# Four modulation vectors of an encoder kernel: one-column products against selector products of split halves

## The chip, the cores and the metric

The kernel runs on one core of a Trainium2 chip. Its engines work side by side, each with its own queue: the PE (TensorE, matrix products into PSUM; its weight loads are listed apart as PEld), DVE (VectorE), ACT (ScalarE), POOL (GpSimd) and SP, whose queue issues nearly all transfers (DMA) between the chip's memory and the on-chip buffers. The metric is the device time of one execution in microseconds (us); lower is better.

## The reference

The reference is a trunk of two layers on 256 tokens of width 2048, all in float32. Each layer makes six vectors of 2048 from the conditioning vector c:

```
mod = (silu(c) @ w_mod[l] + b_mod[l])  ->  shift_m, scale_m, gate_m, shift_f, scale_f, gate_f
h = layer_norm(x) * (1 + scale_m) + shift_m          # first modulation
y = concat(four mixers of h @ w_in[l]) @ w_out[l]
x = layer_norm(ALPHA * x + (1 + gate_m) * y)
h = layer_norm(x) * (1 + scale_f) + shift_f          # second modulation
y = conv_ffn(h, ...)                                  # up (2 x 5632), short conv, silu, down
x = layer_norm(ALPHA * x + (1 + gate_f) * y)
```

w_mod of a layer is 2048 x 12288, so the modulation is a product of one row with a large matrix: much memory traffic for little arithmetic.

## The kernel before

**Products.** The weights arrive in float32 and are split into two float32r halves, high and low: ACT casts to the high half `whi` (line 455), DVE subtracts it from the raw weights to get the low half `wlo` (line 456). The activations are split in the same way (`split`, lines 475 and 476). Three products then stand in for one of float32: high by high, high by low, low by high. Some weights are left whole (`wexact`, loaded at line 433) and multiplied in float32. The raw weights use four buffers (`raw`), the halves four buffers of 128 x 1024 under the tag `whi` and four under `wlo`; whole weights take buffers of these two tags in turn, or spare ones (`slot`).

**Stages.** Layer 0 begins with its first modulation in pieces, mixed with its first projections. Each layer then runs the mixers, the output projection (`out_proj`, PSUM tiles `o`), the up projection (`g_c`, `v_c`) and the down projection (`out_proj` again, PSUM tiles `d`). `out_proj` works in three chunks of 1024, 512 and 512 columns. In the last chunk the products of the last four units are kept back and run for token tile 0 first and for token tile 1 second, so that the norm of token tile 0 can begin while the PE still works on token tile 1. `second` (lines 734 to 762) is that norm for token tile 0, `norm` the one for token tile 1. `to_hT` then casts the normalised tokens (`xn`), transposes them on the PE (line 594) and applies scale and shift (`hF`). Its cast carries a dependency on the instructions that finished the scale and the shift (`MOD_BY`). `first_group` runs the first products of the next stage on whole weights: its first unit of weights is loaded ahead of the kept-back products, the three others behind them.

**Modulation.** DVE accumulates each vector over 16 steps: an accumulator of 128 x 2048 (`macc`) gets the raw block of w_mod times one column of silu(c) (`mod_step`, line 250). What is left is the sum over the 128 partitions. `mod_stream` feeds these steps between the units of the main products at rates fixed by hand (`RATES`). When a vector's steps are through, it waits in the list `late` until `settle` sums it:

- gates go to `gate_rows`: split halves, multiplied by a block of ones;
- layer 1's second shift and scale go to `mod_rows`: split halves multiplied by selectors (128 x 4 with one column of ones, `onesR` behind its first 128 columns), which put the sum of column block j into row j of one PSUM tile `ps_row`. The row is copied (`mrow`, line 227), turned by four transposes (line 230), and added to the bias on DVE (line 232);
- all others go to `mod_cols`: a product of the bias columns with the identity, then one float32 product with a single column of ones per block of 128, with the accumulator's block as the stationary operand (`ps_mod`, line 83), and a copy on ACT (lines 207 and 86).

The vectors that are needed at the start of a norm (`WITH_NORM`: layer 0's second shift and scale, layer 1's first shift and scale) are not settled inside the stream but by `need`, called from `before()` at the end of `out_proj`'s last chunk:

```
if before is not None:
    before()
for t in range(2):
    finish(t, state["ps"], c0)
    (norm if t == 1 or then is None else second)(t)
```

Layer 0's second shift and scale are accumulated in two parts: 12 blocks of 128 columns ahead of this place, the other four later.

**Order.** The program states the work in this order; a planner then fixes each engine's queue ahead of the run from its own cost estimates, taking an instruction earlier where an engine would stand idle and its inputs and a buffer are at hand. All products of the kernel are recorded under line 83, so the tiles' names tell them apart.

Of the kernel before, what the change touches and what calls it, by code (L numbers as in the profile page):

```python
# [8 lines left out]
F32R = mybir.dt.float32r  # L9
# [4 lines left out]
P = 128  # L14
# [4 lines left out]
KT = D // P  # L19
# [12 lines left out]
SHIFT_M, SCALE_M, GATE_M, SHIFT_F, SCALE_F, GATE_F = range(6)  # L32
# [22 lines left out]
def encoder_kernel(ctx: ExitStack, tc: tile.TileContext, A: dict, consts: bass.AP, out: bass.AP):  # L55
# [5 lines left out]
    splitp = ctx.enter_context(tc.tile_pool(name="splitp", bufs=4))  # L61
# [11 lines left out]
    def tmp_tile(name):  # L73
        return tmpp.tile([P, 512], F32, tag="tmp", name=name)

    def ms_tile(name):
        return msp.tile([P, 512], F32, tag="ms", name=name)
# [4 lines left out]
    def mm(o, lhsT, rhs, start, stop):  # L82
        pe.matmul(o, lhsT, rhs, start=start, stop=stop, skip_group_check=True)  # L83
# [21 lines left out]
    onesR = keep.tile([P, P + 16], F32R, name="onesR")  # L105
# [50 lines left out]
    bcol = []  # L156
# [41 lines left out]
    def mod_cols(l, m, k0, acc):  # L198

        n = acc.shape[1] // P  # L200
        ps = ms_tile("ps_mod")
        mm(ps[:, 0:n], ident, bcol[l][:, m * KT + k0 : m * KT + k0 + n], True, False)
        for j in range(n):
            mm(ps[:, j : j + 1], acc[:, j * P : (j + 1) * P], ones[:, 0:1], False, True)
        cols = keep.tile([P, n], F32, name=f"mod_{l}_{m}_{k0}")
        if m in (SHIFT_M, SHIFT_F):
            done = act.copy(cols, ps[:, 0:n])
        else:
            done = ident_act(cols, ps[:, 0:n], 1.0, ones[:, 0:1])
        for j in range(n):  # L210
            MOD[(l, m, k0 + j)] = cols[:, j : j + 1]
            MOD_BY[(l, m, k0 + j)] = done.ins.name

    def halves(acc, c0):
        hi = splitp.tile([P, 1024], F32R, tag="whi", name="mhi")
        lo = splitp.tile([P, 1024], F32R, tag="wlo", name="mlo")
        split((hi, lo), acc[:, c0 : c0 + 1024])
        return [(hi[:, i * 512 : (i + 1) * 512], lo[:, i * 512 : (i + 1) * 512]) for i in range(2)]

    def mod_rows(l, m, acc):  # L220

        ps = ms_tile("ps_row")
        for j, pair in enumerate(halves(acc, 0) + halves(acc, 1024)):
            for n, part in enumerate(pair):
                mm(ps[0:4, :], onesR[:, P + 4 * j : P + 4 * j + 4], part, j + n == 0, j + n == 4)
        row = tmp_tile("mrow")
        act.copy(row[0:4, :], ps[0:4, :])
        ps = ms_tile("ps_mod")
        for i in range(4):
            pe.transpose(ps[:, 4 * i : 4 * i + 4], row[0:4, i * P : (i + 1) * P], ident[0:4, 0:4])  # L230
        cols = keep.tile([P, KT], F32, name=f"mod_{l}_{m}")
        done = dve.scalar_tensor_tensor(
            out=cols.rearrange("p (i j) -> p i j", i=4),
            in0=ps[:, 0:KT].rearrange("p (i j) -> p i j", i=4),
            scalar=0.0 if m == SHIFT_F else 1.0,
            in1=bcol[l][:, m * KT : (m + 1) * KT].rearrange("p (j i) -> p i j", i=4),
            op0=ALU.add,
            op1=ALU.add,
        )
        for k in range(KT):  # L240
            at = 4 * (k % 4) + k // 4
            MOD[(l, m, k)] = cols[:, at : at + 1]
            MOD_BY[(l, m, k)] = done.ins.name
# [39 lines left out]
    def gate_rows(l, m, acc):  # L283

        g = keep.tile([P, D], F32, tag="gate", name=f"gate_{l}_{m}")
        for h in range(2):
            for i, (hi, lo) in enumerate(halves(acc, h * 1024)):
                c0 = h * 1024 + i * 512
                ps = ms_tile("ps_gate")
                mm(ps, onesR[:, 0:P], hi, True, False)  # L290
                mm(ps, onesR[:, 0:P], lo, False, True)
                ident_act(g[:, c0 : c0 + 512], ps, 1.0, ones[:, 0:1])
        GATE[(l, m)] = g
# [5 lines left out]
    def settle(i=0):  # L299
        l, m, acc, k0, k1 = late.pop(i)  # L300
        if m in (GATE_M, GATE_F):
            gate_rows(l, m, acc)
        elif (l, m) in ((1, SHIFT_F), (1, SCALE_F)):
            mod_rows(l, m, acc)
        else:
            mod_cols(l, m, k0, acc[:, k0 * P : k1 * P])

# [15 lines left out]
    def mod_stream(order):  # L323
# [4 lines left out]
        for l, m in order:  # L328
# [10 lines left out]
            while len(late) >= 2:  # L339
                if late[0][:2] in WITH_NORM:  # L340
                    yield
                else:
                    settle()
# [5 lines left out]
            for kt in range(KT):  # L349
                raw = raw_tile("wmod")  # L350
                nc.sync.dma_start(out=raw[:, :w], in_=A["w_mod"][l, kt * P : (kt + 1) * P, m * D : m * D + w])
                if kt == KT - 1 and m in (GATE_M, GATE_F):
                    row = raw_tile("brow")
                    nc.sync.dma_start(out=row[0:1, :], in_=A["b_mod"][l : l + 1, m * D : (m + 1) * D])
                mod_step(acc[:, :w], raw[:, :w], kt, kt == 0)
                if kt == KT - 1:
                    if m in (GATE_M, GATE_F):
                        dve.tensor_tensor(out=acc[0:1, :], in0=acc[0:1, :], in1=row[0:1, :], op=ALU.add)
                    late.append((l, m, acc, 0, k1))
                yield  # L360
                if kt == 1 and late and late[0][:2] not in WITH_NORM:
                    settle()
# [16 lines left out]
    def need(l, m, k1=KT):  # L379
        while (l, m, k1 - 1) not in MOD and (l, m) not in GATE:  # L380
            at = [i for i, x in enumerate(late) if x[:2] == (l, m) and x[4] == k1]
            if at:
                settle(at[0])
            else:
                assert next(mods, "end") != "end"
# [87 lines left out]
    def split(dst, src):  # L473
        hi, lo = dst[:2]
        act.copy(hi, src)  # L475
        dve.tensor_tensor(out=lo, in0=src, in1=hi.bitcast(F32), op=ALU.subtract)  # L476
# [1142 lines left out]
```

## Time and profile before

| | |
|---|---|
| median of 3 runs | 2282.78 us (2282.72 to 2288.62) |
| profiled execution, its own time | 2281.42 us |
| its span | 2279.7 us |
| mean granted PE clock | 0.991 |
| PE, DVE, ACT busy | 98%, 78%, 48% of the span |
| memory traffic | 605.21 MB, mean 265 GB/s |

The times are those of whole executions; the profile is one execution of its own, and the span is what its trace covers. In rows of the timeline the first number is the start in us from the span's start, the second the length, then engine, line, operation, output and inputs by tile names, and the number of instructions merged; in brackets stands the idle time of the engine before them and what ended it. Rows of groups give the shortest, median and longest duration in ns. "PEclk" is the granted clock of the PE as a share of full speed. Under each of the four calls in question: the product of the bias and the one-column products of layer 0's second shift ran from 340.88, its scale's from 393.30, layer 1's first shift's from 1038.82, its first scale's from 1118.58.

### The profile page before, as it was taken

The page shows a single profiled execution, that of the slowest core. Times are in us where ns is not written, and L with a number is a line of the kernel's source. Part 1 is how long each engine was busy: PE and PEld are TensorE (multiplying, and loading weights), DVE is VectorE, ACT ScalarE, POOL GpSimd, SP SyncE. Part 2 cuts the span into 40 slices and gives each one's busy share as a digit, 9 for nine tenths or more (in the row PEclk, how much of TensorE's full clock was granted, in tenths as well). Part 3 has the DMA queues.
Part 4 walks back from the last instruction along what each step waited for, and adds up shares of the span by engine and source line. Part 5 has one row for each costly group of instructions (what it writes and reads, how often), then busy time and mean ns, then how long its engine had stood idle before and what let it go on. Part 6 is the DMA issues. An engine that isn't in the chain of part 4 may idle for free.

```text
span 2279.7 us, 31503 instructions
## 1 busy us (share of the span) xinstructions
PE 2238.7 (98%) x12387; PEld 1934.8 (85%) x12387; DVE 1773.3 (78%) x2183; ACT 1098.2 (48%) x1644; POOL 35.1 (2%) x65
## 2 busy tenths in 40 slices
PE   7999999999999999999999999999999999999998
PEld 5788886798888888888789999889888888888886
DVE  5778988888888888988977899787676565565776
ACT  3356641354455444544454434545544454454553
POOL 0011000000000000000000000000000000000000
PEclk9999999999999999999999999999999999999999
DMA  9999699778888888898777677775666555555554
GB/s 349 385 373 359 256 328 349 249 278 314 311 307 315 314 312 327 303 346 302 273 236 254 201 242 250 271 273 177 240 240 215 192 185 197 191 185 194 187 191 148
DMA packets 228717, 605.21 MB, mean 265 GB/s; under 512 B 14660, under 2 KB 27188, under 8 KB 210900
## 3 DMA queue, kind: packets, MB, share of 16 engines
q1 hardware_dynamic: 227784, 602.30, 74.3%
q8 instruction: 97, 1.59, 0.3%
q0 software_dynamic: 784, 0.90, 0.1%
q14 instruction: 52, 0.43, 0.0%
HBM read 601.05 MB, written 2.10 MB: 265 GB/s over the span
## 4 chain that ended last, share of the span: by engine, by line
PE 88%; DVE 7%; DMA 2%; ACT 2%; issue 1%; POOL 0%; SPq 0%; DVEq 0%; ACTq 0%; POOLq 0%
PE g_c L83 22%; PE v_c L83 22%; PE d L83 20%; PE o L83 7%; PE D_c L83 3%; PE C_c L83 3%; PE B_c L83 2%; PE U_c L83 1%; PE E L83 1%; PE E_c L83 1%; DVE wlo L456 1%; PE ps_mod L83 1%; PE V L83 1%; DVE qacc L250 1%; DVE macc L250 1%
## 5 line engine op out<-in xcount | busy, mean ns | idle before, releaser
L455 ACT CAST whi<-wraw 128x1024 fp32r<-128x1024 f32 (+1 forms) x632 | 643.4, 1043 | 753.1 <-PE g_c L83 217.0
L456 DVE TENSOR_TENSOR wlo<-wraw,whi 128x1024 fp32r<-128x1024 f32 (+1 forms) x632 | 750.5, 1214 | 294.3 <-ACT whi L455 273.2
L83 PE MATMUL d<-whi,a 128*128 128x512 f32 x1344 | 390.3, 391 | 0.9 <-ACT whi L455 0.9
L250 DVE SCALAR_TENSOR_TENSOR macc<-wmod,cact,macc 128x2048 f32<-128x2048 f32 (+2 forms) x174 | 353.9, 2034 | 41.5 <-DMA wmod<-in_w_mod_dram 40.8
L83 PE MATMUL v_c<-hT,whi 128*128 128x512 f32 (+1 forms) x1456 | 343.1, 383 | 0.0
L83 PE MATMUL g_c<-hT,whi 128*128 128x512 f32 (+1 forms) x1344 | 313.5, 380 | 0.0
L83 PEld LDWEIGHTS v_c<-hT,whi 128*128 128x128 f32 x1456 | 264.6, 189 | 48.5
L83 PEld LDWEIGHTS d<-whi,a 128*128 128x128 f32 x1344 | 253.4, 189 | 54.5 <-ACT whi L455 2.2
L83 PEld LDWEIGHTS g_c<-hT,whi 128*128 128x128 f32 x1344 | 243.4, 189 | 43.5 <-DVE second L1436 0.4
L83 PE MATMUL d<-wlo,a 128*128 128x512 f32 x672 | 234.8, 392 | 1.6 <-DVE wlo L456 1.6
L83 PE MATMUL v_c<-hT,wlo 128*128 128x256 f32 x1400 | 190.7, 283 | 0.0
L83 PEld LDWEIGHTS v_c<-hT,wlo 128*128 128x128 f32 x1400 | 183.1, 191 | 6.6
L83 PE MATMUL g_c<-hT,wlo 128*128 128x256 f32 x1280 | 175.8, 283 | 0.0
L83 PEld LDWEIGHTS g_c<-hT,wlo 128*128 128x128 f32 x1280 | 168.2, 191 | 5.9
L83 PEld LDWEIGHTS d<-wlo,a 128*128 128x128 f32 x672 | 126.7, 189 | 30.1 <-DVE wlo L456 3.6
L475 ACT CAST a<-g 128x512 fp32r<-128x512 f32 x132 | 80.8, 619 | 91.1 <-PE d L83 89.4
L83 PE MATMUL o<-whi,a 128*128 128x512 f32 x384 | 111.3, 395 | 0.2 <-ACT whi L455 0.2
L476 DVE TENSOR_TENSOR a<-g,a 128x512 fp32r<-128x512 f32 x132 | 87.7, 684 | 9.2 <-ACT a L475 9.2
L250 DVE SCALAR_TENSOR_TENSOR qacc<-wmod,cact,qacc 128x1024 f32<-128x1024 f32 (+1 forms) x75 | 80.3, 1071 | 12.2 <-DMA wmod<-in_w_mod_dram 9.9
L83 PEld LDWEIGHTS o<-whi,a 128*128 128x128 f32 x384 | 72.7, 190 | 16.4 <-issue 0.7
L83 PE MATMUL D_c<-hT,whi 128*128 128x256 f32 x432 | 83.0, 292 | 2.4 <-ACT hT L475 1.6
L83 PEld LDWEIGHTS D_c<-hT,whi 128*128 128x128 f32 x432 | 69.5, 197 | 4.8 <-ACT hT L475 1.7
(370 smaller groups left out, 2619.1 us busy)
## 6 DMA issues: line engine op xcount, KB each, us to landing
wraw<-in_ffn_w_up_dram SPq DMA_DIRECT2D x168, 1024.0 KB, 5.0
wmod<-in_w_mod_dram SPq DMA_DIRECT2D x134, 1024.0 KB, 6.8
wraw<-in_ffn_w_down_dram SPq DMA_DIRECT2D x88, 1024.0 KB, 5.1
wraw<-in_w_in_dram SPq DMA_DIRECT2D x33, 1024.0 KB, 6.1
wmod<-in_w_mod_dram SPq DMA_DIRECT2D x64, 512.0 KB, 9.4
wraw<-in_w_out_dram SPq DMA_DIRECT2D x26, 1024.0 KB, 6.9
wmod<-in_w_mod_dram SPq DMA_DIRECT2D x32, 768.0 KB, 7.5
wexact<-in_w_in_dram SPq DMA_DIRECT2D x46, 512.0 KB, 7.9
```

What stands on the lines that cost most here:

```text
L83: pe.matmul(o, lhsT, rhs, start=start, stop=stop, skip_group_check=True)
L250: i = dve.scalar_tensor_tensor(out=acc, in0=w, scalar=col, in1=acc, op0=ALU.mult, op1=ALU.add)
L455: act.copy(hi[:, :m], r)
L456: i = dve.tensor_tensor(out=lo[:, :m], in0=r, in1=hi[:, :m].bitcast(F32), op=ALU.subtract)
L475: act.copy(hi, src)
L476: dve.tensor_tensor(out=lo, in0=src, in1=hi.bitcast(F32), op=ALU.subtract)
```

## The change

`mod_rows` takes a number n of 512-column blocks (4 or 3), `halves` a width. `settle` now sends every late vector that starts at block 0 and is not a gate through `mod_rows`. That moves four calls from `mod_cols`: layer 1's first shift and scale (16 blocks each) and the first 12 blocks of layer 0's second shift and scale. The last four blocks of the latter and layer 0's first modulation stay with `mod_cols`. Per moved call the bias product, the 16 or 12 one-column products and the copy on ACT go; two casts and two subtractions (the second of 512 columns for 12 blocks), eight or six selector products, a copy of 4 x 512, four transposes and one addition on DVE come.

```diff
--- before.py
+++ after.py
@@ -211,18 +211,19 @@
             MOD[(l, m, k0 + j)] = cols[:, j : j + 1]
             MOD_BY[(l, m, k0 + j)] = done.ins.name
 
-    def halves(acc, c0):
-        hi = splitp.tile([P, 1024], F32R, tag="whi", name="mhi")
-        lo = splitp.tile([P, 1024], F32R, tag="wlo", name="mlo")
-        split((hi, lo), acc[:, c0 : c0 + 1024])
-        return [(hi[:, i * 512 : (i + 1) * 512], lo[:, i * 512 : (i + 1) * 512]) for i in range(2)]
-
-    def mod_rows(l, m, acc):
+    def halves(acc, c0, width=1024):
+        hi = splitp.tile([P, 1024], F32R, tag="whi", name="mhi")[:, :width]
+        lo = splitp.tile([P, 1024], F32R, tag="wlo", name="mlo")[:, :width]
+        split((hi, lo), acc[:, c0 : c0 + width])
+        return [(hi[:, i : i + 512], lo[:, i : i + 512]) for i in range(0, width, 512)]
+
+    def mod_rows(l, m, acc, n=4):
 
         ps = ms_tile("ps_row")
-        for j, pair in enumerate(halves(acc, 0) + halves(acc, 1024)):
-            for n, part in enumerate(pair):
-                mm(ps[0:4, :], onesR[:, P + 4 * j : P + 4 * j + 4], part, j + n == 0, j + n == 4)
+        parts = [x for c0 in range(0, n * 512, 1024) for x in halves(acc, c0, min(1024, n * 512 - c0))]
+        for j, pair in enumerate(parts):
+            for i, part in enumerate(pair):
+                mm(ps[0:4, :], onesR[:, P + 4 * j : P + 4 * j + 4], part, j + i == 0, j + i == n)
         row = tmp_tile("mrow")
         act.copy(row[0:4, :], ps[0:4, :])
         ps = ms_tile("ps_mod")
@@ -230,14 +231,14 @@
             pe.transpose(ps[:, 4 * i : 4 * i + 4], row[0:4, i * P : (i + 1) * P], ident[0:4, 0:4])
         cols = keep.tile([P, KT], F32, name=f"mod_{l}_{m}")
         done = dve.scalar_tensor_tensor(
-            out=cols.rearrange("p (i j) -> p i j", i=4),
-            in0=ps[:, 0:KT].rearrange("p (i j) -> p i j", i=4),
-            scalar=0.0 if m == SHIFT_F else 1.0,
-            in1=bcol[l][:, m * KT : (m + 1) * KT].rearrange("p (j i) -> p i j", i=4),
+            out=cols.rearrange("p (i j) -> p i j", i=4)[:, :, :n],
+            in0=ps[:, 0:KT].rearrange("p (i j) -> p i j", i=4)[:, :, :n],
+            scalar=0.0 if m in (SHIFT_M, SHIFT_F) else 1.0,
+            in1=bcol[l][:, m * KT : m * KT + 4 * n].rearrange("p (j i) -> p i j", i=4),
             op0=ALU.add,
             op1=ALU.add,
         )
-        for k in range(KT):
+        for k in range(4 * n):
             at = 4 * (k % 4) + k // 4
             MOD[(l, m, k)] = cols[:, at : at + 1]
             MOD_BY[(l, m, k)] = done.ins.name
@@ -300,8 +301,8 @@
         l, m, acc, k0, k1 = late.pop(i)
         if m in (GATE_M, GATE_F):
             gate_rows(l, m, acc)
-        elif (l, m) in ((1, SHIFT_F), (1, SCALE_F)):
-            mod_rows(l, m, acc)
+        elif k0 == 0:
+            mod_rows(l, m, acc, k1 // 4)
         else:
             mod_cols(l, m, k0, acc[:, k0 * P : k1 * P])
```

## The prediction

> **What bounds the kernel now.** I read the page's busy times and chain first.
>
> ```profile
> span 2279.7 us, 31503 instructions
> PE 2238.7 (98%) x12387; PEld 1934.8 (85%) x12387; DVE 1773.3 (78%) x2183; ACT 1098.2 (48%) x1644; POOL 35.1 (2%) x65
> PE 88%; DVE 7%; DMA 2%; ACT 2%; issue 1%; POOL 0%; SPq 0%; DVEq 0%; ACTq 0%; POOLq 0%
> ```
>
> PE is the bound: busy for 98% of the span, and 88% of the chain of waits. So the question for each of the four calls is what the PE loses on it today and what it will lose afterwards. Then I cut the time around the four calls into stretches. The view of stretches gives length, then busy time and number of instructions for PE, PEld, DVE, ACT and POOL, then the granted PE clock and the DMA share. The first row is plain layer-0 down projection, then come layer 1's first shift, its scale, layer 0's second shift, its scale.
>
> ```profile
> 1027.90:1038.80 10.90, 10.90 (x49) 9.02 (x49) 10.47 (x9) 5.04 (x6) 0.00 (x0) 1.00 0.97 355
> 1038.80:1043.90 5.10, 5.10 (x42) 4.86 (x41) 1.83 (x2) 0.65 (x2) 0.00 (x0) 1.00 0.90 320
> 1043.90:1047.50 3.60, 3.60 (x11) 2.88 (x11) 2.48 (x3) 2.03 (x3) 0.00 (x0) 0.56 0.71 277
> 1118.57:1122.26 3.69, 3.69 (x34) 3.65 (x32) 3.69 (x5) 2.11 (x3) 0.00 (x0) 1.00 0.71 295
> 1122.26:1126.30 4.04, 4.04 (x13) 3.18 (x13) 2.41 (x3) 2.15 (x3) 0.00 (x0) 0.58 0.81 262
> 340.85:344.10 3.25, 3.25 (x30) 3.18 (x28) 2.31 (x3) 1.86 (x2) 0.00 (x0) 1.00 0.99 392
> 344.10:347.70 3.60, 3.60 (x11) 2.85 (x11) 3.56 (x3) 0.24 (x2) 0.00 (x0) 0.57 0.97 361
> 393.30:396.30 3.00, 3.00 (x26) 2.76 (x25) 2.96 (x6) 0.00 (x0) 0.00 (x0) 1.00 1.05 406
> 396.30:400.00 3.70, 3.70 (x11) 1.79 (x11) 1.75 (x5) 0.27 (x1) 0.00 (x0) 1.00 1.05 389
> ```
>
> A plain 512-column product takes 10.90/49 = 0.22 us. A burst of one-column products costs twice: its own time, and in three of four cases a granted clock of 0.56 to 0.58 for about 3.7 us behind it.
>
> **What is removed.** Per call, the burst less the ordinary products that fall into the stretch (0.22 each), plus the lost clock:
> - layer 1 shift: 42 records, 36 of them the call's (32 one-column, 4 of the bias); 5.10 - 6 x 0.22 = 3.8, and 3.60 x 0.44 = 1.6: 5.4 us.
> - layer 1 scale: 32 of 34; 3.69 - 0.44 = 3.25, and 4.04 x 0.42 = 1.7: 4.95 us.
> - layer 0 shift: 28 of 30; 3.25 - 0.44 = 2.8, and 3.60 x 0.43 = 1.55: 4.35 us.
> - layer 0 scale: 24 of 26, some 2.9 us, no lost clock.
>
> Together 17.6 us of PE time. Not all comes back, because something else would have made the PE wait:
>
> ```profile
> 340.71 1.99 ACT L455 CAST whi<-wraw 128x1024 fp32r<-128x1024 f32 x2 [6.12 <-DMA wraw<-in_w_out_dram]
> 347.63 2.00 ACT L455 CAST whi<-wraw 128x1024 fp32r<-128x1024 f32 x2 [3.36 <-DMA wraw<-in_w_out_dram]
> 1119.36 2.35 DVE L456 TENSOR_TENSOR wlo<-wraw,whi 128x1024 fp32r<-128x1024 f32 x2
> 1122.29 0.77 PE L83 MATMUL d<-whi,a 128*128 128x512 f32 x2
> 1045.02 2.36 DVE L456 TENSOR_TENSOR wlo<-wraw,whi 128x1024 fp32r<-128x1024 f32 x2 [4.38 <-ACT whi L455]
> ```
>
> These are rows of the timeline (start, length, engine, what, idle time before and who ended it). Layer 0's shift lies where the casts wait for weights from memory (DMA share 0.97 to 0.99): the next unit's raw weights land at 347.63 whatever the PE does, so I take 1.5 of 4.35 (ends 0 and 4.35). At layer 1's scale the products after the burst need the low half whose first subtraction ends at 1119.36 + 1.18 = 1120.54; they start at 1122.29, so 1.75 comes back, with 1.7 of clock: 3.4 (ends 1.7 and 4.95). At layer 1's shift nothing else was late (the DVE itself sat idle for 4.38 us behind it): all 5.4. Layer 0's scale stands on the chain of waits:
>
> ```profile
> 379.96 13.93 PE o L83 x55
> 393.89 2.57 PE ps_mod L83 x24
> 396.46 20.72 PE o L83 x48
> ```
>
> so its 2.9 is counted in full (lower end 0, if the next exact weights were late). Returned: 5.4 + 3.4 + 1.5 + 2.9 = 13.2 us, of at most 17.6.
>
> **What is added.** The same helper already runs for layer 1's second shift and scale, so every piece has a row: cast and subtraction of a 1024-column half, selector product, copy of the row, transposes, the add.
>
> ```profile
> L475 ACT CAST mhi<-macc x12: 1029/1052/1057, 256.3 to 2146.5; 128x1024 fp32r<-128x1024 f32 x12
> L476 DVE TENSOR_TENSOR mlo<-macc,mhi x12: 1205/1220/1226, 260.2 to 2147.6; 128x1024 fp32r<-128x1024 f32 x12
> L83 PE MATMUL ps_row<-mhi,onesR x8: 391/396/397, 774.7 to 915.6; 128*4 128x512 f32 x8
> L227 ACT COPY mrow<-ps_row x2: 567/567/567, 780.1 to 916.8; 4x512 f32<-4x512 f32 x2
> 780.77 0.41 PE L230 MATMUL ps_mod<-cst,mrow 4*128 4x4 f32 x4
> L232 DVE SCALAR_TENSOR_TENSOR mod<-ps_mod,bcol x2: 173/174/174, 781.3 to 918.3; 128x16 f32<-128x16 f32 x2
> 910.00:920.00 10.00, 10.00 (x59) 7.92 (x59) 8.21 (x15) 7.03 (x13) 0.00 (x0) 1.00 0.56 208
> ```
>
> The selector product streams 512 columns, so pipelined it costs the same 0.22 us as its neighbours, and around the present calls the clock stays at 1.00. On the PE a call of 16 blocks costs 8 x 0.22 + 0.41 = 2.2 us, one of 12 blocks 6 x 0.22 + 0.41 = 1.7 us: 7.8 us for all four. ACT gets two casts (2.1 us) and a 0.57 copy per call, DVE two subtractions (2.4 us) and a 0.17 add; I estimate a 512-column half at half of these.
>
> **Where it will run** decides more than these sums. One-column products needed only an accumulator and a PSUM buffer, and the order of issue had moved them ahead: they are written behind the last chunk of the projection, yet layer 1's shift ran at 1038.8, about 150 us before that place. The halves need a pair of the four high and four low weight buffers, for which the weight stream always queues. The last gate goes through the same buffers:
>
> ```profile
> 1711.59 2.27 DVE L358 TENSOR_TENSOR macc<-macc,brow 1x2048 f32<-1x2048 f32 x1
> 2145.14 1.05 ACT L475 CAST mhi<-macc 128x1024 fp32r<-128x1024 f32 x1 [2.51 <-PE d L83]
> 2147.53 1.05 ACT L455 CAST whi<-wraw 128x1024 fp32r<-128x1024 f32 x1
> ```
>
> Its accumulator was ready at 1713.9, its first cast ran at 2145.14 at its written place, when a product released a buffer. So I expect the four calls to stay at theirs: the end of layer 0's output projection and of its down projection, where the first normalised tile waits for them. The second of these ends so:
>
> ```profile
> 1186.59 5.65 SPq L433 DMA_DIRECT2D wexact<-in_w_in_dram  x8
> 1190.47 0.39 PE L83 MATMUL d<-whi,a 128*128 128x512 f32 x1
> 1190.57 1.52 ACT L86 ACTIVATE xn<-x,rs_d0r 128x512 f32<-128x512 f32 x2 [1.70 <-DVE rs_d0r L762]
> 1191.44 1.36 PE L594 MATMUL ps_xT<-cst,xn 128*128 128x128 f32 x8 [0.58 <-ACT xn L86]
> ```
>
> Call the end of the last product T (1190.9). The last two units hold all the pairs and release them in steps of six products, 1.36 us: at T-4.1 (taken by the next stage's first exact weights), T-2.7 and T-1.36 (the shift's halves), T (the scale's first). The scale's second follows once the shift's products (from T, 0.9 us each half) have released one. Its cast waits for ACT until T+1.05 and ends at T+2.1; its subtraction follows the scale's first (T+2.3) until T+3.5; four products to T+4.4; copy, transposes and add 1.15, and some 0.5 of handing over, to T+6.1. The cast to the normalised tile, which carries a dependency on both vectors, ran at T; it is 6.1 us late, and the PE has little else. On SP, six of the eight exact loads move behind the halves by some 5 us; the products that read them move by 6.1, so that is covered. DVE's norm of token tile 0 ran until T; the subtractions in its way (2.4 us before T) are covered by the same 6.1. Token tile 1's norm has 12 us of PE work before it is needed.
>
> At the output projection two of the last four units use other buffers, so more pairs are free. I take both shift halves as hidden (DVE idles 8.79 us there) and the scale's second half as the late one: products, copy, transposes and add, T+3.0 (ends 0 and 6.1).
>
> ```profile
> 406.91 0.69 DVE L701 TENSOR_TENSOR yg<-o,gate 128x512 f32<-128x512 f32 x1 [8.79 <-PE o L83]
> 429.79 0.66 PE L594 MATMUL ps_xT<-cst,xn 128*128 128x128 f32 x4 [0.79 <-ACT xn L86]
> ```
>
> Of it 0.8 disappears in a wait of the PE for token tile 1 at 429.79: 2.2 us.
>
> The sum: -13.2 + 6.1 + 2.2 = -4.9 us. The profiled execution took 2281.42 us (span 2279.7), so 2276.5; the median shown is 2282.78, 1.4 above it, so 2278 for the median.
>
> The Trainium skill, "TensorE: Matmul & The Clock Gate", section "Part 1: The HAM clock gate", says that an idle window of about 3.4 us puts the array back to half clock, which speaks against the change: at T+3.5 to T+7 the PE is almost idle. By it the sum would be 1.7 us higher, by the stretch from 1122.26. No row of the trace before shows such a gap at a seam, so the sum leaves it out.
>
> **The rivals.**
> - Clean swap: the calls still run inside the stream, with nothing lost at the ends and nothing covered: -17.6 + 7.8 = -9.8, so 2271.6, 2273 for the median. For it: casts of the next chunk came behind the gate's at 2147.53, so the halves can win buffers. Against it: the 430 us that the gate waited.
> - The DVE takes it back: the calls run in the stream and the subtractions delay the weights. In the first row quoted DVE is busy for 10.47 of 10.90 us. -13.2 + 7.8 + 4 x 1.22 = -0.5: 2282 for the median. Against it: after the scale's last step no accumulation follows until the norm.
> - Slower: one pair of buffers only. If the next stage's exact loads take every pair as it comes free, the halves go one after the other, each waiting for the products of the one before: 1.05 + 1.22 + 4 x 0.22 = 3.15 us a half. Down projection 4 x 3.15 + 1.15 - 1.4 (begun before T) = 12.4, output projection 2 x (3.15 + 1.6) + 1.15 = 10.6; 23.0 - 13.2 = +9.8, 2292.6 for the median. It decides from the point where fewer than two pairs are free at T. For it: the exact loads need no engine, only the buffer (eight issued in 5.65 us from 1186.59). Against it: they are written behind the halves.
>
> **How the numbers follow.** Forecast 0.41, clean swap 0.28, DVE 0.16, one pair 0.15. A measurement of this kernel can tell about 0.3%, 6.8 us, from no change. Faster: most of the clean swap (0.26) and the upper gains of the forecast, where layer 0's covers are thin (0.08). Slower: 0.14. Same: the rest, 0.52. The range reaches from 4 us under the clean swap (other covers gone) to 2288, where one seam goes one half at a time; what it leaves out is the full one-pair case and a little below.
>
> **What would show it.** No stretch with a clock near 0.57 at 344, 1044 and 1122. The casts of the accumulators at the two ends of projections, one waiting for a product to release its buffer; were they near 341, 1039 and 1118 instead, the step on the buffers is wrong. The first normalised tile waiting for the add of the scale, 2 to 6 us after the last product; a wait of over 10 us means one pair. More DVE-caused waits of the PE in layer 0's down projection mean the DVE rival. Were the down projection not about 8 us shorter, the returned PE time is wrong.

## The result and the profile after

The changed kernel takes 2302.3 us (median of 6 runs, 2298.66 to 2307.37); the kernel before took 2283.4 us beside it (6 runs, 2282.72 to 2288.62). The ratio is 1.0078 with a 95% interval of 1.0062 to 1.0093: about 19 us slower, where the prediction said 5 us faster and ended its range at 2288. The profiled execution of the changed kernel took 2301.58 us, with a span of 2299.8, 20.1 over the span before, at a mean granted clock of 0.988 (before: 0.991).

From the page of the changed kernel: span, busy times, shares of the chain of waits.

```profile
span 2299.8 us, 31392 instructions
PE 2233.8 (97%) x12311; PEld 1925.0 (84%) x12311; DVE 1780.1 (77%) x2195; ACT 1106.2 (48%) x1652; POOL 35.1 (2%) x65
PE 86%; DVE 8%; DMA 3%; issue 2%; ACT 1%; POOL 0%; SPq 0%; DVEq 0%; ACTq 0%; POOLq 0%
```

The PE is busy for 4.9 us less than before, although the span is 20.1 us longer. So the PE did have less to do, and about 25 us of idle PE came instead. Where, the groups by form show: each of the next four rows has a first or last start that marks the end of a stage. Kernel before (ns shortest/median/longest, then first and last start in us):

```profile
L83 PE MATMUL o<-wexact,yd x16: 592/592/592, 403.3 to 416.6; 128*128 128x512 f32 x16
L83 PE MATMUL g_c<-hF,wexact x480: 275/275/764, 419.1 to 1558.9; 128*128 128x128 f32 x149, 128*128 128x256 f32 x11
L83 PE MATMUL d<-thi,a x64: 389/389/389, 1168.9 to 2262.5; 128*128 128x512 f32 x64
L83 PE MATMUL U_c<-hF,wexact x256: 275/275/377, 1192.6 to 1223.8; 128*128 128x128 f32 x128
```

The same groups of the changed kernel:

```profile
L83 PE MATMUL o<-wexact,yd x16: 592/592/593, 397.2 to 410.5; 128*128 128x512 f32 x16
L83 PE MATMUL g_c<-hF,wexact x480: 274/275/763, 428.4 to 1579.0; 128*128 128x128 f32 x149, 128*128 128x256 f32 x11
L83 PE MATMUL d<-thi,a x64: 389/389/390, 1169.6 to 2282.6; 128*128 128x512 f32 x64
L83 PE MATMUL U_c<-hF,wexact x256: 275/275/574, 1210.1 to 1242.1; 128*128 128x128 f32 x128
```

The last `o` product ends layer 0's output projection, the first `g_c` is the next stage; the first `d<-thi` stands in the last kept-back products of layer 0's down projection, the first `U_c` is the start of layer 1. The differences of these marks cut the span into five stretches. The two columns on the right are experiments that come below.

| stretch (us) | before | after, difference | norm first | summed early |
|---|---|---|---|---|
| start to last `o` | 416.6 | -6.1 | -6.1 | -0.3 |
| last `o` to first `g_c` (first end) | 2.5 | +15.4 | +5.6 | 0.0 |
| first `g_c` to first `d<-thi` | 749.8 | -8.6 | -9.4 | -3.5 |
| first `d<-thi` to first `U_c` (second end) | 23.7 | +16.8 | +7.4 | 0.0 |
| first `U_c` to the end of the span | 1087.1 | +2.6 | +1.8 | 0.0 |
| span | 2279.7 | +20.1 | -0.7 | -3.8 |

The streams of products did become shorter, by 14.7 us. The two ends of projections, at which the first normalised tile is awaited, became longer by 32.2 us.

Each column is one profiled execution, and the first stretch varies: in the three experiments below whose first stretch has the one-column products of the kernel before (the wait alone, and layer 1's pair alone in either place) it is 418.1 to 420.1 us, 1.5 to 3.5 longer than before. The changed kernel's 410.5 did repeat (410.5 and 410.3 in the two that share its first stretch). So did the ends: in the two experiments that move only one layer's pair, each end is within 0.2 us of its length in the kernel before or in the changed kernel.

What happens at the second end, in the timeline of the changed kernel:

```profile
1188.80 1.05 ACT L476 CAST mhi<-macc 128x1024 fp32r<-128x1024 f32 x1 [11.58 <-PE d L83]
1189.88 5.08 DVE L477 TENSOR_TENSOR mlo<-macc,mhi 128x1024 fp32r<-128x1024 f32 x4 [11.22 <-ACT mhi L476]
1191.32 0.40 PE L83 MATMUL ps_row<-mhi,onesR 128*4 128x512 f32 x1
...
1194.97 0.68 DVE L702 TENSOR_TENSOR yg<-d,gate 128x512 f32<-128x512 f32 x1
...
1197.52 0.18 DVE L233 SCALAR_TENSOR_TENSOR mod<-ps_mod,bcol 128x16 f32<-128x16 f32 x1 [1.87 <-PE ps_mod L231]
1197.61 0.68 DVE L705 SCALAR_TENSOR_TENSOR x<-x,yg 128x512 f32<-128x512 f32 x1
...
1201.54 0.72 ACT L747 ACTIVATE sq<-x,c_d 128x512 f32<-128x512 f32 x1 [4.52 <-DVE x L738]
...
1207.52 2.23 ACT L86 ACTIVATE xn<-x,rs_d0r 128x512 f32<-128x512 f32 x3 [1.71 <-DVE rs_d0r L763]
...
1208.39 1.97 PE L595 MATMUL ps_xT<-cst,xn 128*128 128x128 f32 x8 [10.91 <-ACT xn L86]
```

The projection's products end at 1191.32, where the first selector product starts. Call it T; the prediction took T from the end of the last product's row, which by the same rule would be 1191.48 here, 0.16 later. DVE sat idle for 11.22 us ahead of its first subtraction (`mlo`), because the cast that feeds it (`mhi`) came late: ACT had been idle for 11.58 us ahead of that cast, until a product released a weight buffer. The norm of token tile 0 (`yg`, then `x<-x,yg`, and so on) stands behind the subtractions, and its second step behind the scale's add as well. The same two steps in the kernel before:

```profile
1180.02 0.69 DVE L701 TENSOR_TENSOR yg<-d,gate 128x512 f32<-128x512 f32 x1 [1.97 <-PE d L83]
1180.74 0.69 DVE L704 SCALAR_TENSOR_TENSOR x<-x,yg 128x512 f32<-128x512 f32 x1
```

There `yg` began as soon as token tile 0's products were through, and the norm ran under token tile 1's products. Its length is unchanged: from `x<-x,yg` to the cast `xn` it was 1190.57 - 1180.74 = 9.8 us, and is 1207.52 - 1197.61 = 9.9. Only now all of it lies behind T, with an idle PE. ACT's queue was not the later limit: ACT sat idle until DVE's step had run, and its first square (`sq`) came 1201.54 - 1197.61 = 3.9 us after `x<-x,yg`, as it did before (1184.68 - 1180.74). The first end has the same picture:

```profile
406.01 0.62 ACT L476 CAST mhi<-macc 128x512 fp32r<-128x512 f32 x1 [16.12 <-PE o L83]
...
416.19 0.17 DVE L233 SCALAR_TENSOR_TENSOR mod<-ps_mod,bcol 128x12 f32<-128x12 f32 x1 [1.79 <-PE ps_mod L231]
416.28 0.68 DVE L705 SCALAR_TENSOR_TENSOR x<-x,yg 128x512 f32<-128x512 f32 x1
...
426.65 0.69 PE L595 MATMUL ps_xT<-cst,xn 128*128 128x128 f32 x2 [10.50 <-ACT xn L86]
```

The view of stretches of the changed kernel (columns as in the prediction: length, then PE, PEld, DVE, ACT, POOL, then granted clock and DMA share), with three stretches around the places of the old one-column products and the two ends:

```profile
335.00:360.00 25.00, 23.60 (x100) 18.24 (x99) 20.70 (x17) 6.00 (x6) 0.00 (x0) 1.00 0.96 354
1020.00:1060.00 40.00, 40.00 (x178) 33.11 (x178) 34.98 (x28) 17.75 (x21) 0.00 (x0) 1.00 0.96 359
1100.00:1130.00 30.00, 29.06 (x127) 23.23 (x126) 30.00 (x32) 16.25 (x21) 0.00 (x0) 1.00 0.88 326
415.00:426.60 11.60, 0.49 (x5) 0.32 (x4) 9.32 (x26) 4.45 (x11) 1.55 (x2) 0.71 0.64 230
426.60:428.40 1.80, 1.75 (x8) 1.57 (x8) 1.70 (x5) 1.80 (x5) 0.08 (x1) 0.50 0.00 0
428.40:430.00 1.60, 1.60 (x9) 1.59 (x8) 1.60 (x3) 1.60 (x6) 0.91 (x1) 0.50 0.05 10
430.00:433.00 3.00, 3.00 (x28) 3.00 (x27) 3.00 (x6) 0.79 (x3) 0.00 (x0) 0.97 0.00 0
1208.30:1214.60 6.30, 6.21 (x40) 6.03 (x41) 6.20 (x12) 4.92 (x12) 0.93 (x1) 0.72 0.01 3
```

The three stretches of low clock behind the one-column products, 0.56 to 0.58 near 344, 1044 and 1122, are gone: the first three rows stand at 1.00. At the first end the PE is busy for 0.49 of 11.60 us while DVE works for 9.32, and when the PE starts again its clock is at 0.50 for 3.4 us: 1.8 us more (1.80 x 0.50 + 1.60 x 0.50 + 3.00 x 0.03). The second end loses as much: 6.30 x 0.28 = 1.8. Of each 1.8, half lies ahead of the mark that closes the end (the first `g_c`, the first `U_c`) and half behind it.

### The profile page after: what moved, and what is told of

The parts are those of the page before. It is cut to its first block, busy times and chain, and to the rows that moved or that the text cites. A ratio compares the mean times of both kernels' runs of the same rounds, so it can differ in the third digit from the quotient of the medians.

```text
span 2299.8 us, 31392 instructions
## 1 busy us (share of the span) xinstructions
PE 2233.8 (97%) x12311; PEld 1925.0 (84%) x12311; DVE 1780.1 (77%) x2195; ACT 1106.2 (48%) x1652; POOL 35.1 (2%) x65
## 4 chain that ended last, share of the span: by engine, by line
PE 86%; DVE 8%; DMA 3%; issue 2%; ACT 1%; POOL 0%; SPq 0%; DVEq 0%; ACTq 0%; POOLq 0%
PE g_c L83 22%; PE v_c L83 21%; PE d L83 19%; PE o L83 6%; PE D_c L83 3%; PE C_c L83 3%; PE B_c L83 2%; DVE wlo L457 1%; PE U_c L83 1%; DVE macc L251 1%; PE E L83 1%; DMA wmod<-in_w_mod_dram 1%; PE E_c L83 1%; DVE qacc L251 1%; PE U L83 1%
```

## The experiments

Three theories, named by letters in some of the expectations. A: the order in DVE's queue; the subtractions and the adds stand ahead of token tile 0's norm, and because they wait for the other tile's products, the norm does too. B: the weights' buffers; that the halves wait for them, and the weights for the halves, makes the loss by itself. C: the planner gave the whole program another order, and the loss is spread. All kernels were timed in three rounds against the kernel before. Its median was 2283.70 us beside the norm first, layer 1's pair alone, the wait alone and the sums earlier, and 2283.18 beside the other four.

**The norm ahead of the sums.** The changed kernel, with the call of `before()` behind token tile 0's norm:

```diff
-                if before is not None:
-                    before()
                 for t in range(2):
                     finish(t, state["ps"], c0)
                     (norm if t == 1 or then is None else second)(t)
+                    if t == 0 and before is not None:
+                        before()
```

> The changed kernel, with the four calls written behind token tile 0's norm instead of ahead of it (the call of before() moves into the loop, behind second(0)); same work, same buffers. Theory A (DVE's queue): the halves' subtractions and the two adds stand ahead of token tile 0's norm in DVE's queue and hold it until the last product; so here the norm runs under token tile 1's products again, the PE's waits of 10.5 and 10.9 us for the first normalised tile shrink to some 6 us less the row products, and the time falls by about 9 us a seam, to 2283 to 2286 us. Theory B (buffers: the vectors and the next exact weights are late because the halves get their buffers only at the end): the vectors come no sooner, the waits stay, 2300 us or more.

Measured: 2282.91 us, ratio to before 0.9993 (0.9981 to 1.0005). The whole loss is gone by moving one call past one norm; the time lies at the edge of the 2283 to 2286 that theory A expected, and B's 2300 is excluded. Its marks:

```profile
L83 PE MATMUL o<-wexact,yd x16: 592/592/592, 397.2 to 410.5; 128*128 128x512 f32 x16
L83 PE MATMUL g_c<-hF,wexact x480: 275/275/764, 418.6 to 1558.1; 128*128 128x128 f32 x149, 128*128 128x256 f32 x11
L83 PE MATMUL d<-thi,a x64: 389/389/389, 1159.0 to 2261.8; 128*128 128x512 f32 x64
L83 PE MATMUL U_c<-hF,wexact x256: 275/275/422, 1190.1 to 1223.0; 128*128 128x128 f32 x128
```

With its span of 2279.0 they give the column "norm first" above. The ends still cost 13.0 us (5.6 + 7.4), because the sums are still late. From its timeline at the second end:

```profile
1187.81 0.17 DVE L233 SCALAR_TENSOR_TENSOR mod<-ps_mod,bcol 128x16 f32<-128x16 f32 x1 [2.09 <-PE ps_mod L231]
1188.08 1.52 ACT L86 ACTIVATE xn<-x,rs_d0r 128x512 f32<-128x512 f32 x2 [0.77 <-DVE mod L233]
1188.94 1.36 PE L595 MATMUL ps_xT<-cst,xn 128*128 128x128 f32 x8 [1.17 <-ACT xn L86]
```

Now the cast `xn` waits for the scale's add and follows it at once, as the prediction had it for the change; in the changed kernel it came 10 us behind that add.

**Layer 1's pair alone** in the written place, layer 0's by one-column products:

```diff
-        elif k0 == 0:
+        elif k0 == 0 and l == 1:
             mod_rows(l, m, acc, k1 // 4)
```

> The changed kernel with layer 0's pair back on one-column products; layer 1's pair by selector products. If each end of a projection pays for its own pair, the first end is as before and the rest keeps its ledger: about 9.4 us less in the down projection, 17 us more at its end, 2 to 3 us more behind it: 2283.4 + 10 = 2293 us. If the loss came from a new order of the whole program (rival C), it would be all or nothing: near 2283 or near 2302.

Measured: 2293.91 us, ratio 1.0038 (1.0022 to 1.0053), 10.2 us over the kernel before.

**Layer 0's pair alone:**

```diff
-        elif k0 == 0:
+        elif k0 == 0 and (l == 0 or m in (SHIFT_F, SCALE_F)):
             mod_rows(l, m, acc, k1 // 4)
```

> Only layer 0's two vectors by selectors, layer 1's first two by one-column products as before. In the changed kernel's trace the end of the output projection came 6.1 us earlier and the first gate product 9.3 us later than before, so by the theory that the first token tile's norm is queued on DVE behind the halves at each end, this kernel is some 9 us (9.3 at that end, less or more 2) over the kernel before: 2292 to 2294. Together with layer 1's pair alone (10.2 us over) that would be the whole loss of 19. A theory in which the loss is made jointly (both pairs contending for the same buffers, or an order of the whole program that shifts) expects less than 5 us here: under 2288.

Measured: 2293.11 us, ratio 1.0053 (1.0037 to 1.0069), 9.9 us over before. 10.2 and 9.9 make 20.1, beside a loss of 19: each end loses by itself, and no joint loss shows beyond the few us of the intervals. That speaks against C.

**The wait alone.** The kernel before, with a copy of one element of token tile 1's result on DVE, and token tile 0's first step ordered behind it; no sum is changed:

```diff
                 if before is not None:
                     before()
+                    box["wait"] = dve.tensor_copy(
+                        smallp.tile([P, 2], F32, tag="mv", name="probe", bufs=4)[:, 0:1], state["ps"][1][0][:, 0:1])
...
                 i = dve.tensor_tensor(out=y, in0=p, in1=box["gate"][:, cols], op=ALU.mult)
+                if t == 0 and "wait" in box:
+                    tc.add_manual_dep(i.ins, box["wait"].ins.name, order_dep, reason="the wait under test")
```

> The kernel before, with one tiny DVE copy out of token tile 1's finished sum put ahead of token tile 0's norm at both ends; one-column products, no halves. Only DVE's wait for the last product is added. Theory A: the norm of 10.3 us is laid bare at both ends, and the clock falls behind the PE's idle time: 2283.4 + 2 x 10 to 12 = 2303 to 2308 us. Theory B: nothing is late for buffers here, 2283 to 2286 us.

Measured: 2319.65 us, ratio 1.0141 (1.0109 to 1.0172), 36 us over before: the direction of A, but 12 us beyond its bound. The groups of the probe and the timeline show why:

```profile
L854 DVE COPY probe<-o x2: 159/159/159, 418.8 to 1550.2; 128x1 f32<-128x1 f32 x2
L854 DVE COPY probe<-d x1: 159/159/159, 1202.6 to 1202.6; 128x1 f32<-128x1 f32 x1
```
```profile
429.90 1.97 PE L594 MATMUL ps_xT<-cst,xn 128*128 128x128 f32 x8 [11.13 <-ACT xn L86]
...
1214.11 1.97 PE L594 MATMUL ps_xT<-cst,xn 128*128 128x128 f32 x8 [11.54 <-ACT xn L86]
...
1561.30 1.97 PE L594 MATMUL ps_xT<-cst,xn 128*128 128x128 f32 x8 [11.13 <-ACT xn L86]
```

The probe ran three times, not two: the end of layer 1's output projection goes through the same lines. Each time the PE waited some 11 us for the first cast, 36 / 3 = 12 us an end with the clock. So the order of DVE's queue alone, without any sum, makes the loss of an end; the expectation's error was the count.

**Other buffers for the halves.** The changed kernel, whose four moved calls take their halves from four small scratch buffers:

```diff
-        parts = [x for c0 in range(0, n * 512, 1024) for x in halves(acc, c0, min(1024, n * 512 - c0))]
+        parts = []
+        if (l, m) in ((1, SHIFT_F), (1, SCALE_F)):
+            parts = halves(acc, 0) + halves(acc, 1024)
+        else:
+            for j in range(n):
+                hi = tmpp.tile([P, 512], F32R, tag="tmp", name="mhi")
+                lo = tmpp.tile([P, 512], F32R, tag="tmp", name="mlo")
+                split((hi, lo), acc[:, j * 512 : (j + 1) * 512])
+                parts.append((hi, lo))
```

> The four calls stay where they are written, but their halves take 512 columns each in four small scratch buffers, so they no longer wait for the weights' halves. In each engine's fixed queue the subtractions and the shift's add still stand ahead of the first token tile's norm on DVE, and on the PE the selector products behind the other token tile's products; with two pairs of small buffers the scale's last subtractions wait for products behind the projection's end. The theory of the queue order expects the loss to stay: 2298 to 2305, with an idle stretch of the PE of some 10 us ahead of the first transposes at both ends. The theory that the weights' buffers as such make the loss expects it to be gone: 2278 to 2284.

Measured: 2308.32 us, ratio 1.0118 (1.01 to 1.0137): the loss stays, 3 us beyond A's range, and B's 2278 to 2284 is excluded. From its timeline at the second end:

```profile
1194.61 0.69 DVE L485 TENSOR_TENSOR mlo<-macc,mhi 128x512 fp32r<-128x512 f32 x1 [13.08 <-PE ps_row L83]
...
1202.84 0.17 DVE L241 SCALAR_TENSOR_TENSOR mod<-ps_mod,bcol 128x16 f32<-128x16 f32 x1 [1.24 <-PE ps_mod L239]
1202.93 0.68 DVE L713 SCALAR_TENSOR_TENSOR x<-x,yg 128x512 f32<-128x512 f32 x1
...
1213.71 1.97 PE L603 MATMUL ps_xT<-cst,xn 128*128 128x128 f32 x8 [10.92 <-ACT xn L86]
```

The subtraction no longer waits for a weight buffer but for a selector product, which stands on the PE behind token tile 1's products. With another thing to wait for, DVE's queue holds the norm back as it did: `x<-x,yg` again follows the scale's add at once. The add itself ends 5.3 us later than in the changed kernel (1203.01 against 1197.70).

**The sums earlier.** The changed kernel with `before()` at the start of the last chunk, ahead of the kept-back products:

```diff
-                if before is not None:
-                    before()
                 for t in range(2):
...
+                if last and u == 0 and before is not None:
+                    before()
                 if last and u >= units - 4:
                     state["tail"].append((item, u))
```

> The changed kernel, with the four calls written at the start of the projection's last chunk, ahead of the kept-back products. Theory A: no subtraction stands ahead of the norm at the ends, the bursts and the low clock stay gone: about -15.5 (measured on the way to the two ends) + 7.8 for the row products = 2276 us, faster than both. Theory B: the halves take buffers from the weight stream instead, and the weights are late: 2283 to 2290 us.

Measured: 2277.21 us, ratio 0.9963 (0.995 to 0.9977), faster than both kernels. Its span is 2275.9, and its marks are

```profile
L83 PE MATMUL o<-wexact,yd x16: 592/592/593, 403.0 to 416.3; 128*128 128x512 f32 x16
L83 PE MATMUL g_c<-hF,wexact x480: 275/275/766, 418.8 to 1555.2; 128*128 128x128 f32 x149, 128*128 128x256 f32 x11
L83 PE MATMUL d<-thi,a x64: 389/389/389, 1165.1 to 2258.8; 128*128 128x512 f32 x64
L83 PE MATMUL U_c<-hF,wexact x256: 275/275/377, 1188.8 to 1220.0; 128*128 128x128 f32 x128
```

Both ends are back at their length of before (2.5 and 23.7). The selector products now cost their PE time in the stream, and nothing else comes with them at the down projection: 8.6 to 9.4 us returned, by the two columns, less 2 x 2.2 us of the prediction's price is 4.2 to 5.0, and 3.5 was measured. In the first stretch only 0.3 of a possible 6.1 - 3.4 = 2.7 us stayed, but that stretch varies by more than this without the change (1.5 to 3.5 us, as said under the table), so the 0.3 tells little.

**Early, with layer 1's pair alone** (the edit of the second experiment on top of this kernel):

> As the kernel that sums at the start of the last chunk, but layer 0's pair by one-column products. In that kernel's trace the last product of layer 0's output projection started at 416.3 (before: 416.6), and the first gate product at 418.8 (before: 419.1): layer 0's pair gained nothing there, and the whole gain of some 6 us came in layer 1's pair. So the theory that layer 0's output projection waits for weights from memory whatever the PE does expects the same time, 2276 to 2279. If layer 0's returned PE time counted (4 us of it), this kernel would be at 2281.

Measured: 2280.26 us, ratio 0.9987 (0.9977 to 0.9997), outside the 2276 to 2279 that was expected and near the 2281 of the other theory. In the profiled executions the stretch from the first `o` to the first `g_c` is 105.6 us here, 104.4 with both pairs early, and 105.4 before. So layer 0's pair seems to bring something, about 1 us in these traces; by the medians it is 3, with intervals of the ratios that touch at 0.9977. Its size stays open.

**Early, with scratch buffers** (both edits):

> Both: small scratch buffers for the halves, and the sums written at the start of the last chunk, ahead of the kept-back products. Nothing queued for weights' buffers and nothing ahead of the norm: the clean swap of the prediction, 2272 to 2276, if the weights' buffers still cost something in the kernel that sums early (2277.2). If those buffers cost nothing there, 2276 to 2278.

Measured: 2276.08 us, ratio 0.9974 (0.9965 to 0.9984), not to be told from the early sums with the weights' buffers (0.995 to 0.9977). With the sums early, the weights' buffers cost nothing that these runs can show.

## Why the prediction was wrong

- **Returned PE time: right in size.** 13.2 us predicted; 14.7 in the changed kernel (6.1 + 8.6), 15.5 with the norm first (6.1 + 9.4). Both are net of the low clock behind the first `g_c`, which cost 0.9 and 1.7 us there. The low clock behind the one-column products is gone, as the rows from 335, 1020 and 1100 show. One term is off by its own rule: layer 0's scale is 3.00 - 2 x 0.22 = 2.6, not 2.9, which makes the sum 12.9.
- **Where the calls run: right.** They stayed at the two ends, and the first cast of each waited for a product to release a buffer (11.58 and 16.12 us of idle ACT). The clean swap and the DVE rival, which had them in the stream, fall. The clean swap is what the early sums come near to: 2277.2, where the rival said 2273.
- **When the second end's scale is ready: right.** Predicted T+6.1; the add ended at 1197.70 = T+6.4. The working buffer by buffer held: the casts ran at T-2.5, T-1.2 and T+0.2, where T-2.7, T-1.36 and T were predicted.
- **The step that failed** is one sentence: "DVE's norm of token tile 0 ran until T; the subtractions in its way (2.4 us before T) are covered by the same 6.1." It placed the subtractions inside the norm's time, and took the norm as done at T. But they stand ahead of the norm in DVE's queue, the first of them cannot run before the last units release buffers, and the add of the scale (T+6.4) stands ahead of the norm's second step. So the two times don't cover each other, they follow each other: 6.4 to the add, then 9.9 of norm. The transposes, 0.5 behind T before (1191.44 against 1190.9), are 17.1 behind T (1208.39 against 1191.32). The prediction asked what moves behind the halves on SP, but looked at DVE's work only as time to be covered, not as a queue.
- **The two ends in the sum:** 6.1 + 2.2 = 8.3 predicted, 32.2 measured. With the norm first they are 13.0, so the queue order makes 19.2 of the difference; 1.7 of that is low clock ahead of the two marks. The remaining 4.7 are two terms that were sized too small, for with the norm first the clock stood at 1.00 up to both marks: the second end was 7.4 in place of 6.1, the first 5.6 in place of 2.2 (3.0, less a cover of 0.8 that would show behind the mark). At the first end "I take both shift halves as hidden" was too hopeful. In the changed kernel the shift's selector products ran behind the projection's, from 410.56, and the scale's behind the shift's transposes, from 413.52, so the scale's add ended at 416.36, 5.4 us after the projection's products and not 3.0.
- **The clock at the ends: left out, and it should have stood in the sum.** With the rows at 0.50 the trace agrees with the rule that the prediction cited from the Trainium skill, "TensorE: Matmul & The Clock Gate", section "Part 1: The HAM clock gate": half clock after an idle window of about 3.4 us. At the first end the PE's last instruction ended at 416.16, and the clock was 1.00 up to 419 and 0.50 from 420. The prediction's 1.7 us were measured as 1.8, at both ends. It dropped the term because the trace before had no such gap, yet its own timeline made one.
- **Cover on SP: right as far as the marks tell.** The changed kernel's `U_c` products start 17.5 us later than before and end 18.3 later. The 0.8 is about the low clock behind the first `U_c` (0.9), which leaves nothing for the delayed exact loads.
- **The slower rival** (one pair of buffers) had the right direction, and the PE's wait of over 10 us that it was to be known by did appear, but not for its reason: the halves did not go one by one, since the sums were ready at T+6.4, against 12.4 by that rival. Its 2292.6 was near for the wrong reason.
- **Behind the second end:** of the 2.6 us that the changed kernel loses after the first `U_c`, 0.9 is the rest of the low clock at that end, and 1.7 is one more stretch of low clock in layer 1. The kernel before has one such stretch there (1428 to 1435, clock 0.76), the changed kernel two (1350 to 1356 and 1545 to 1551, both 0.72), each worth 1.7 us. Why the changed kernel has one more was not tested.

## What to carry to other kernels

When a step is given inputs that come late (a buffer, a product), ask for every engine that it runs on what stands behind it in that engine's queue, and whether that is on the path: two things that seem to cover each other add up if they share a queue. Here 19 us of loss and 6 us of gain differ only in where one call is written: behind the kept-back products, or ahead of them. A saving inside the stream is worth little until the place at which its replacement runs has been priced.

## What the runs showed of the hardware

The granted clock fell without a long idle stretch of the PE. With the norm first, the PE's longest waits at the first end were about 1.2 us, but in the last 2.6 us it was busy for only half of the time, with the scale's transposes and those of the normalised tile. The view of stretches of that kernel:

```profile
416.00:418.60 2.60, 1.36 (x12) 0.95 (x10) 2.25 (x6) 2.03 (x4) 0.29 (x1) 1.00 1.04 368
418.60:422.00 3.40, 3.40 (x20) 3.40 (x19) 3.40 (x7) 3.10 (x8) 0.70 (x1) 0.57 1.02 377
422.00:425.00 3.00, 3.00 (x26) 3.00 (x26) 3.00 (x6) 0.46 (x2) 0.00 (x0) 0.92 1.05 391
...
1190.10:1192.00 1.90, 1.90 (x12) 1.85 (x11) 1.90 (x4) 1.90 (x6) 0.77 (x1) 0.60 1.02 385
1192.00:1196.00 4.00, 4.00 (x29) 4.00 (x29) 4.00 (x7) 1.94 (x4) 0.00 (x0) 0.76 0.56 199
```

A stretch of 2.6 us that was busy for 52% is followed by a clock of 0.57 for 3.4 us: 1.7 us lost (3.40 x 0.43 + 3.00 x 0.08), about as much as behind the 11 us of almost nothing in the changed kernel. At the second end it is the same 1.7 (1.90 x 0.40 + 4.00 x 0.24). So the loss was the same for a sparse stretch as for a long gap. That the sparseness is the cause isn't shown: the prediction's rows have the same low clock behind one-column products with the PE busy throughout. Nor does such a burst always bring it. Layer 1's mixers have two, of 20 products (`ps_ss`) and 16 (`ps_var`), with the same work in both kernels; before, only the second was followed by low clock (the stretch from 1428), after the change only the first (the stretch from 1350).
